# MLP products by one level of Strassen's algorithm, with the hidden activations kept in DRAM

## The chip, the core and the metric

One core of a Trainium2 chip runs the whole kernel. TensorE multiplies matrices out of SBUF into PSUM; VectorE (DVE), ScalarE (ACT) and GpSimd (POOL) work on tiles elementwise; SyncE (SP) issues most of the DMAs. The metric is the device time of one execution in microseconds, the median of several runs.

## What is computed

Two layers of a diffusion block on 512 latent and 256 context tokens of 1024 features in float32. Each layer has a mixer (recurrence, attention, pooling) and then the part that is changed, the MLP:

```python
def _mlp(h, w1, w2):
    return jnp.square(jax.nn.relu(h @ w1)) @ w2
...
        x = x + g2 * _mlp(_modulate(_rmsnorm(x, g_norm2[l]), sh2, sc2), w_ff1[l], w_ff2[l])
        if not last:
            h = h + cg1 * y_ctx
            h = h + cg2 * _mlp(_modulate(_rmsnorm(h, g_norm2[l]), csh2, csc2), w_ff1[l], w_ff2[l])
```

w_ff1 is 1024 x 4096 and w_ff2 4096 x 1024. Layer 0 carries 768 tokens through it, layer 1 (the last) only the 512 latent ones.

## The kernel before

Features lie on partitions, tokens in columns. Every float32 operand of a product is kept as two float32r parts, high (a cast) and low (the operand minus its high part), and a product is three matmuls: high x high, high x low, low x high (`mm3`, L241 is its matmul). The weights come as blocks of 128 x 1024 in the order of their use; `Weights.advance` loads a block ("raw"), ScalarE casts it to "whi" (L142) and VectorE subtracts to get "wlo" (L143).

`ffn(l)` runs the MLP in four groups of eight hidden chunks of 128 features. `ff1` makes a chunk: 8 feature tiles x 3 matmuls x 2 column segments (512 and 258 in layer 0; 256 and 258 in layer 1, two further columns carrying the shift), then VectorE multiplies by the tokens' 1/rms ("tf", L539), ScalarE takes ReLU (L544, L546) and the square ("hh", L1255), VectorE squares again and subtracts ("r" L1256, "hl" L1257). The hidden chunks stay in SBUF. `ff2` multiplies a group's eight chunks into each of the eight output tiles and VectorE adds the gated result to the residual tile "xo" out of PSUM (L1276). Both layers' `ffn` are straight code; a scheduler orders each engine's instructions, and each engine then runs its own in order.

Beside this, `mod_rows` (L413, "junk") computes the modulation of the next layer on VectorE, a row block at a time for both streams; these items ("fill") are spread over layer 0's MLP. In the mixer's tail ("wo" products, `add_to` L1189, `scaled` L467 and L468) GpSimd adds up squares ("acc", L456).

## Time and profile before

| | |
|---|---|
| median of 3 runs | 1652.8 us (1650.26 to 1652.82) |
| span of the profiled execution (the page gives no other time for it) | 1650.7 us |
| TensorE busy | 1582.8 us |
| VectorE busy | 1122.0 us |
| ScalarE busy | 680.4 us |
| GpSimd busy | 368.2 us |
| bytes read from and written to HBM | 170.90 and 12.12 MB |

Busy time is an average over stages with different limits, so the stages are read one by one: mixer of layer 0 up to 443 us, its MLP to 984, mixer of layer 1 to 1283, its MLP to the end. Only the last link of a chain of waits costs time.

### The profile page before, as it was taken

The page shows a single profiled execution, that of the slowest core. Times are in us where ns is not written, and L with a number is a line of the kernel's source. Part 1 is how long each engine was busy: PE and PEld are TensorE (multiplying, and loading weights), DVE is VectorE, ACT ScalarE, POOL GpSimd, SP SyncE. Part 2 cuts the span into 40 slices and gives each one's busy share as a digit, 9 for nine tenths or more (in the row PEclk, how much of TensorE's full clock was granted, in tenths as well). Part 3 has the DMA queues.
Part 4 walks back from the last instruction along what each step waited for, and adds up shares of the span by engine and source line. Part 5 has one row for each costly group of instructions (what it writes and reads, how often), then busy time and mean ns, then how long its engine had stood idle before and what let it go on. Part 6 is the DMA issues. An engine that isn't in the chain of part 4 may idle for free.

```text
span 1650.7 us, 24064 instructions
## 1 busy us (share of the span) xinstructions
PE 1582.8 (96%) x9519; PEld 1380.6 (84%) x9519; DVE 1122.0 (68%) x1810; ACT 680.4 (41%) x1078; POOL 368.2 (22%) x376
## 2 busy tenths in 40 slices
...
GB/s 251 198 150 185 81 58 37 94 185 152 82 97 144 142 89 119 187 78 128 166 90 120 142 109 21 121 71 20 97 122 141 103 90 96 97 90 93 100 27 102
DMA packets 54016, 184.57 MB, mean 112 GB/s; under 512 B 6624, under 2 KB 7264, under 8 KB 53904
## 3 DMA queue, kind: packets, MB, share of 16 engines
...
HBM read 170.90 MB, written 12.12 MB: 111 GB/s over the span
## 4 chain that ended last, share of the span: by engine, by line
PE 76%; DVE 15%; issue 4%; ACT 3%; POOL 1%; DMA 1%; SPq 0%; DVEq 0%; ACTq 0%; POOLq 0%
PE f L241 55%; PE wo L241 5%; PE inps L241 4%; PE sc L241 3%; DVE wlo L143 3%; PE tp L914 2%; DVE p L897 1%; PE modps L369 1%; DVE junk L413 1%; PE qp L241 1%; PE pv L936 1%; PE pv L937 1%; DVE ptl L922 1%; PE gps L241 1%; PE kns L823 1%
## 5 line engine op out<-in xcount | busy, mean ns | idle before, releaser
L142 ACT CAST whi<-raw 128x1024 fp32r<-128x1024 f32 x210 | 219.6, 1048 | 657.2 <-PE f L241 550.7
L143 DVE TENSOR_TENSOR wlo<-raw,whi 128x1024 fp32r<-128x1024 f32 x210 | 276.3, 1318 | 35.3 <-ACT whi L142 32.6
L241 PE MATMUL f<-xh,whi 128*128 128x258 f32 (+2 forms) x1024 | 234.6, 310 | 1.0 <-DVE tf L539 1.0
L241 PE MATMUL f<-xl,whi 128*128 128x258 f32 (+2 forms) x1024 | 234.5, 310 | 0.0
L241 PE MATMUL f<-xh,wlo 128*128 128x258 f32 (+2 forms) x1024 | 234.1, 310 | 0.0
L241 PE MATMUL f<-hh,wlo 128*128 128x512 f32 (+1 forms) x768 | 232.2, 356 | 0.0
L241 PE MATMUL f<-hl,whi 128*128 128x512 f32 (+1 forms) x768 | 231.9, 356 | 0.0
L241 PE MATMUL f<-hh,whi 128*128 128x512 f32 (+1 forms) x768 | 231.3, 356 | 0.0
L1276 DVE SCALAR_TENSOR_TENSOR xo<-f,mod,xo 128x512 f32<-128x512 f32 x96 | 60.5, 658 | 195.6 <-PE f L241 195.6
L413 DVE SCALAR_TENSOR_TENSOR junk<-modraw,cb 128x1024 bf16<-128x1024 f32 x128 | 161.8, 1275 | 21.9 <-DMA modraw<-in_wb_dram 21.5
L241 PEld LDWEIGHTS f<-xh,whi 128*128 128x128 f32 x1024 | 157.8, 189 | 12.5 <-PE f L241 1.2
L241 PEld LDWEIGHTS f<-xl,whi 128*128 128x128 f32 x1024 | 158.2, 189 | 11.4
L241 PEld LDWEIGHTS f<-xh,wlo 128*128 128x128 f32 x1024 | 157.9, 189 | 11.3
L539 DVE TENSOR_TENSOR tf<-f,rb 128x770 f32<-128x770 f32 (+1 forms) x64 | 52.8, 826 | 159.1 <-PE f L241 150.2
L241 PEld LDWEIGHTS f<-hh,whi 128*128 128x128 f32 x768 | 126.5, 188 | 22.4
L241 PEld LDWEIGHTS f<-hh,wlo 128*128 128x128 f32 x768 | 126.3, 188 | 22.5
L241 PEld LDWEIGHTS f<-hl,whi 128*128 128x128 f32 x768 | 126.4, 188 | 22.3
L463 POOL CAST xh<-mod 128x2 fp32r<-128x2 f32 x24 | 10.6, 441 | 466.8 <-PE f L241 466.8
L225 POOL TENSOR_SCALAR p<-p,sm 128x768 f32<-128x768 f32 (+1 forms) x80 | 70.4, 880 | 117.3 <-DVE sm L899 81.1
L241 PE MATMUL inps<-xh,whi 128*128 128x512 f32 (+1 forms) x352 | 87.3, 331 | 7.3 <-ACT xh L467 5.6
L305 ACT ACTIVATE p<-p,sm 128x768 f32<-128x768 f32 (+1 forms) x80 | 68.2, 853 | 57.4 <-DVE p L897 56.8
L241 PE MATMUL inps<-xl,whi 128*128 128x512 f32 (+1 forms) x352 | 86.4, 326 | 3.1 <-DVE xl L468 3.1
...
## 6 DMA issues: line engine op xcount, KB each, us to landing
raw<-in_wb_dram SPq DMA_DIRECT2D x212, 512.0 KB, 3.6
...
```

The source lines that it names most:

```text
L142: nc.scalar.copy(hi, raw)
L143: nc.vector.tensor_tensor(lo, raw, hi.bitcast(F32), ALU.subtract)
L225: return self.nc.gpsimd.tensor_scalar(out, in_, scale, 0.0, ALU.mult, ALU.add)
L241: nc.tensor.matmul(ps, lhsT=a[:, ca], rhs=b[:, cb], start=first and i == 0, stop=last and i == 2)
L305: ins = self.nc.scalar.activation(out, in_, func, **kw)
L369: nc.tensor.matmul(ps[0:4, :], lhsT=self.ct[:, kk * 2 + j, :], rhs=w[:, j * 512:(j + 1) * 512], start=(kk == 0 and j == 0 and i == 0), sto ...
L413: nc.vector.scalar_tensor_tensor(junk, r, 1.0, c, ALU.mult, ALU.mult, accum_out=acc[l, g][:, v * 16 + i:v * 16 + i + 1])
L539: nc.vector.tensor_tensor(t[:, 0:n], ps[:, o:o + n], self.rb[:, 0:n], ALU.mult)
L823: nc.tensor.matmul(ps[:, tt:tt + 7:6], lhsT=sq[:, tt * 128:(tt + 1) * 128], rhs=self.cst[:, CST_SELK:CST_SELK + 2], start=True, stop=True)
L897: nc.vector.tensor_scalar(p[:, 0:keys], s, rq[:, qt:qt + 1], None, ALU.mult, ALU.min, accum_out=nb)
L914: nc.tensor.transpose(ps[:, j * 256 + q * 128:j * 256 + (q + 1) * 128], ps2[q][:, kt * 128:(kt + 1) * 128], self.ident)
L1276: nc.vector.scalar_tensor_tensor(x[:, a:a + e], ps[:, a:a + e], mod[:, v, 8 + m:9 + m], x[:, a:a + e], ALU.mult, ALU.add)
```

## The change

The MLP's two products are each cut into 2 x 2 blocks: the features of the contraction in halves, the output features in halves, the tokens in halves. A classical product of such blocks takes 8 block products; the new class `FeedForward` takes 7 (Winograd's form of Strassen's algorithm), whose operands are blocks or sums of blocks. Sums and differences are formed in float32, and only then split into high and low part:

- `weight_ops` makes the seven left operands from two raw blocks, "ws" holding the sums. Four sums of 128 x 512 run on GpSimd. Each operand is cast by ScalarE (L1303) and its low part taken (L1304) by VectorE, or by GpSimd for operands 5, 3 and 4 in layer 0 and for 3 in layer 1. `Weights.advance` no longer splits MLP blocks.
- `stream_ops` does the same for activations ("xq" from the scaled x, "hq" from the hidden chunks), sums ("tt") on GpSimd, low parts on VectorE.
- 16 `Hidden` jobs a layer make two hidden chunks each; 8 groups of 4 `Output` jobs make the output, two chunks of either half of the hidden features at a time. A job's seven products are issued as 1, then 3 and 4 of the job before, then 6, 5, 2, 7; the operands of the next job are prepared between them.
- The products are put together while they leave PSUM: some accumulate there, some are copied by ScalarE or added by VectorE to "ya", "yb" or "yo" tiles.
- A hidden chunk, after ReLU and square, is written to DRAM ("hd", by a DMA issued from ScalarE) and read back ("hz") for the second product. x is kept in DRAM too ("xf") and added at the end.
- Modulation rows of the last layer that only the context would use are not computed (`streams`): 80 of the L413 operations fall into layer 0's MLP where 112 did.
- The order of the output projection's tiles becomes 0, 4, 1, 5, 2, 6, 3, 7 (`KORD`), so that tiles which are summed come in pairs.

```diff
-GF = 8
 NSK = 5
 FLOW = (
-    "a2 acc gate hh hl inv knsq latn lsq mix p ps2 pth ptl pvt qlh qll rb t th u yh ylru z",
-    "a2 gate hh hl latn lsq lxp mxl p ps2 pth ptl pvt qlh qll row sq t th u yl ylru z",
+    "a2 acc gate inv knsq latn lsq mix p ps2 pth ptl pvt qlh qll rb t th u yh ylru z xz ya yb rr hz yo tt",
+    "a2 gate latn lsq lxp mxl p ps2 pth ptl pvt qlh qll row sq t th u yl ylru z xz ya yb rr hz yo tt",
 )
 NSLOT, NFLOW = 29, 18
-NGF = D_FF // 128 // GF
+NCH = D_FF // 128
+UNITS = NCH // 2
+UG = 2
+NGROUP = UNITS // UG
+KORD = tuple(j + h * KD // 2 for j in range(KD // 2) for h in range(2))
+FIRST, LATER = (1, 6, 5, 2, 7), (3, 4)
...
+def streams(l, g):
+    return 1 if l == DEPTH - 1 and g else 2
...
-        names += [(l, "ff1", c) for c in range(D_FF // 128)]
-        names += [(l, "ff2", g, m) for g in range(NGF) for m in range(KD)]
+        names += [(l, "ff1", c) for c in range(NCH)]
+        names += [(l, "ff2", g, q, h) for g in range(NGROUP) for q in range(KD // 4) for h in range(2)]
...
+            if name[1] in ("ff1", "ff2"):
+                self.split += 1
+                continue
...
+    def get_raw(self, name):
+        if self.order is None:
+            self.asked.append(name)
+            return FAKE
+        assert self.order[self.at] == name, (self.order[self.at], name)
+        self.loads = 1 if self.order[min(self.at + 4, len(self.order) - 1)][1] in ("ff1", "ff2") else 3
+        self.advance(self.at)
+        self.at += 1
+        return self.raw.pop(name)
...
-            junk = self.sp.tile([128, 1024], BF16, tag="s", name="junk", bufs=NSLOT)
-            for v, c in enumerate(self.cb):
+            junk = self.sp.tile([128, 1024], BF16, tag="f", name="junk", bufs=NFLOW)
+            nv = streams(l, g)
+            for v, c in enumerate(self.cb[:nv]):
                 nc.vector.scalar_tensor_tensor(junk, r, 1.0, c, ALU.mult, ALU.mult,
...
-        def ff1_out(c, ps):
-            t = self.scaled_out(ps, ctx, "tf")
-            r = self.slot("r")
-            self.biased(t, (r[:, 0:L], r[:, L:T]), ctx, AF.Relu)
-            hi, lo = self.slot("hh", F32R), self.slot("hl", F32R)
-            nc.scalar.activation(hi[:, 0:n], r[:, 0:n], AF.Square)
-            nc.vector.tensor_tensor(r[:, 0:n], r[:, 0:n], r[:, 0:n], ALU.mult)
-            nc.vector.tensor_tensor(lo[:, 0:n], r[:, 0:n], hi[:, 0:n].bitcast(F32), ALU.subtract)
-            hid[c] = (hi, lo)
...
-            for j in range(GF):
-                wk = [t[:, j * 128:(j + 1) * 128] for t in w]
-                self.mm3(wk, hid[g * GF + j], segs, j == 0, j == GF - 1)
-            x = self.X[m]
-            mod = self.mod[l, 2].rearrange("p (v j) -> p v j", v=2)
-            for v, a, e in ((0, 0, L), (1, L, C))[:2 if ctx else 1]:
-                nc.vector.scalar_tensor_tensor(x[:, a:a + e], ps[:, a:a + e], mod[:, v, 8 + m:9 + m], x[:, a:a + e],
-                                               ALU.mult, ALU.add)
...
-        self.ffn(1)
+        self.ff.run()
...
+        slow = (5, 3, 4) if self.ctx else (3,)
+        self.low_w = {p: nc.gpsimd if p in slow else nc.vector for p in range(1, 8)}
+        self.jobs = [Hidden(self, u) for u in range(UNITS)]
+        self.jobs += [Output(self, g, m) for g in range(NGROUP) for m in range(KD // 2)]
...
+    def parts(self, hi, lo, src, eng):
+        self.nc.scalar.copy(hi, src)
+        eng.tensor_tensor(lo, src, hi.bitcast(F32), ALU.subtract)
...
+    def stream_ops(self, name, blocks, n, q):
+        nc, sub = self.nc, ALU.subtract
+        t = {}
+        def new(*p):
+            s = self.K.slot("tt")
+            for i, k in enumerate(p):
+                t[k] = s[:, i * n:(i + 1) * n]
+        def part(p, src=None):
+            q[p] = self.K.slot(name, F32R)
+            self.parts(q[p][:, 0:n], q[p][:, n:2 * n], t[p] if src is None else src, nc.vector)
+        def sums():
+            b11, b12, b21, b22 = blocks()
+            new(5, 6)
+            new(7, 4)
+            nc.gpsimd.tensor_tensor(t[5], b12, b11, sub)
+            nc.gpsimd.tensor_tensor(t[6], b22, t[5], sub)
+            nc.gpsimd.tensor_tensor(t[4], b21, t[6], sub)
+            part(6)
+        def third():
+            _, b12, _, b22 = blocks()
+            nc.gpsimd.tensor_tensor(t[7], b22, b12, sub)
+            part(7)
+        return [lambda: part(1, blocks()[0]), sums, lambda: part(5), lambda: part(2, blocks()[2]), third,
+                lambda: part(3, blocks()[3]), lambda: part(4)]
...
+    def weight_ops(self, names, w):
+        nc, K = self.nc, self.K
+        a, t = [], {}
+        def pair(*ps):
+            s = K.rawp.tile([128, 1024], F32, tag="ws", name="ws", bufs=2)
+            for i, p in enumerate(ps):
+                t[p] = s[:, i * 512:(i + 1) * 512]
+        def part(p, src=None):
+            w[p] = K.wp.tile([128, 1024], F32R, tag="w", name="wo")
+            self.parts(w[p][:, 0:512], w[p][:, 512:1024], t[p] if src is None else src, self.low_w[p])
+        def begin():
+            for name in names:
+                r = K.w.get_raw(name)
+                a.extend([r[:, 0:512], r[:, 512:1024]])
+            part(1, a[0])
+        def sums():
+            pair(5, 6)
+            nc.gpsimd.tensor_tensor(t[5], a[2], a[3], ALU.add)
+            nc.gpsimd.tensor_tensor(t[6], t[5], a[0], ALU.subtract)
+            part(6)
+        def third():
+            pair(7, 3)
+            nc.gpsimd.tensor_tensor(t[7], a[0], a[2], ALU.subtract)
+            nc.gpsimd.tensor_tensor(t[3], a[1], t[6], ALU.subtract)
+            part(7)
+        return [begin, sums, lambda: part(5), lambda: part(2, a[1]), third, lambda: part(3), lambda: part(4, a[3])]
...
+    def product(self, ps, p, lhs, rhs, n, start):
+        for i, ((wh, wl), q) in enumerate(zip(lhs, rhs)):
+            xh, xl = q[p][:, 0:n], q[p][:, n:2 * n]
+            for j, (a, b) in enumerate(((wh, xh), (wh, xl), (wl, xh))):
+                self.nc.tensor.matmul(ps, lhsT=a, rhs=b, start=start and i == 0 and j == 0,
+                                      stop=i == len(rhs) - 1 and j == 2, skip_group_check=True)
...
+        total = 7 * UNITS - 14
+        prev = None
+        for i, job in enumerate(self.jobs + [None]):
+            nxt = list(self.jobs[i + 1].prep) if i + 1 < len(self.jobs) else []
+            seq = [(job, p) for p in (FIRST if i else (1, 5, 6, 2, 7))] if job else []
+            late = [(prev, p) for p in LATER] if prev else []
+            seq = seq[:1] + late + seq[1:]
+            for at, (jb, p) in enumerate(seq):
+                jb.do(p)
+                if i == 0 and p == 6:
+                    r = K.norm_sums(self.ctx)
+                if i == 0 and p == 7:
+                    self.norm_spread(r)
+                upto = -(-len(nxt) // (len(seq) - at))
+                for step in nxt[:upto]:
+                    step()
+                del nxt[:upto]
+                ticks += 1
+                while ran < min(fills, -(-fills * ticks // total)):
+                    K.run_fill()
+                    ran += 1
+            prev = job
...
+        ff.product(ps, p, lhs, ff.xq, n, p in (1, 2, 5))
+        half = slice(0, n), slice(n, 2 * n)
+        if p == 1:
+            nc.scalar.copy(self.ya[:, half[0]], ps)
+        elif p == 6:
+            nc.scalar.copy(self.ya[:, half[1]], ps)
+        elif p == 5:
+            nc.scalar.copy(self.yb[:, half[1]], ps)
+        elif p == 2:
+            nc.vector.tensor_tensor(self.ya[:, half[0]], ps, self.ya[:, half[0]], ALU.add)
+        elif p == 7:
+            nc.vector.tensor_tensor(self.yb[:, half[1]], ps, self.yb[:, half[1]], ALU.add)
+        elif p == 3:
+            nc.vector.tensor_tensor(self.ya[:, half[1]], ps, self.ya[:, half[1]], ALU.add)
+            nc.vector.tensor_tensor(self.ya[:, 0:2 * n], self.ya[:, 0:2 * n], ff.rb[:, 0:2 * n], ALU.mult)
+            self.out(self.u, self.ya)
+        else:
+            nc.vector.tensor_tensor(self.yb[:, half[0]], ps, ff.rb[:, half[0]], ALU.mult)
+            nc.vector.tensor_tensor(self.yb[:, half[1]], self.yb[:, half[1]], ff.rb[:, half[1]], ALU.mult)
+            self.out(self.u + UNITS, self.yb)
+    def out(self, c, y):
+        ff, K, nc = self.ff, self.ff.K, self.ff.nc
+        r = K.slot("rr")
+        for at, e, v, t in ff.pieces(2):
+            nc.scalar.activation(r[:, t:t + e], y[:, at:at + e], AF.Relu, bias=y[:, ff.nh + v:ff.nh + v + 1])
+        nc.scalar.activation(r[:, 0:ff.n], r[:, 0:ff.n], AF.Square)
+        nc.scalar.dma_start(out=K.hd[ff.l, c, :, 0:ff.n], in_=r[:, 0:ff.n])
...
+        for t in range(UG):
+            c = (m % 2 * UG + t) * 128
+            lhs.append((self.w[p][:, c:c + 128], self.w[p][:, 512 + c:512 + c + 128]))
+        ff.product(ps, p, lhs, [ff.hq[g * UG + t] for t in range(UG)], n, p in (1, 2, 5))
+        a, b = slice(0, n), slice(n, 2 * n)
+        y, o = {1: (m, a), 6: (m, b), 7: (m + 4, b), 5: (m + 4, b), 2: (m, a), 4: (m + 4, a), 3: (m, b)}[p]
+        y = ff.y[y][:, o]
+        if g == 0 and p in (1, 6, 5, 4):
+            nc.scalar.copy(y, ps)
+        else:
+            nc.vector.tensor_tensor(y, ps, y, ALU.add)
```

GpSimd's instructions in the middle of layer 0's MLP. Before, there are none between the memset of "rb" and the first scaled tiles of the next layer, apart from those of the mixer's last tiles:

```order
L463 CAST xh<-mod_1_975 128x2
L464 TENSOR_TENSOR xl<-mod_1_975,xh 128x2
L507 MEMSET rb 128x2
L463 CAST xh<-mod_1_975 128x2
L464 TENSOR_TENSOR xl<-mod_1_975,xh 128x2
L456 TENSOR_TENSOR acc<-acc,sq 128x768
```

After, the same engine in the first product of layer 0, one job and the start of the next ("ws" are sums of weight blocks, "wo" the split operands):

```order
L1359 TENSOR_TENSOR ws<-raw 128x512
L1365 TENSOR_TENSOR ws<-raw 128x512
L1360 TENSOR_TENSOR ws<-ws,raw 128x512
L1366 TENSOR_TENSOR ws<-raw,ws 128x512
L1304 TENSOR_TENSOR wo<-ws,wo 128x512 x2
L1304 TENSOR_TENSOR wo<-raw,wo 128x512
L1359 TENSOR_TENSOR ws<-raw 128x512
L1365 TENSOR_TENSOR ws<-raw 128x512
```

Seven operations of 512 columns per job stand where the engine had nothing to do.

VectorE in the first product of layer 0, before: one chunk and the start of the next.

```order
L539 TENSOR_TENSOR tf<-f_6098,rb 128x770
L143 TENSOR_TENSOR wlo<-raw,whi 128x1024
L413 SCALAR_TENSOR_TENSOR junk,modr_0_5644<-modraw,cb_1664 128x1024
L1256 TENSOR_TENSOR r<-r 128x768
L413 SCALAR_TENSOR_TENSOR junk,modr_0_5644<-modraw,cb_1665 128x1024
L1257 TENSOR_TENSOR hl<-r,hh 128x768
L539 TENSOR_TENSOR tf<-f_6168,rb 128x770
```

After, one job (two chunks); f is a PSUM tile, every other operand lies in SBUF:

```order
L1472 TENSOR_TENSOR ya<-f_6527,ya 128x386
L1304 TENSOR_TENSOR wo<-raw,wo 128x512
L1474 TENSOR_TENSOR yb<-f_6250,yb 128x386
L1481 TENSOR_TENSOR yb<-yb,rb 128x386
L1476 TENSOR_TENSOR ya<-f_6250,ya 128x386
L1477 TENSOR_TENSOR ya<-ya,rb 128x772
L1304 TENSOR_TENSOR wo<-ws,wo 128x512
L1304 TENSOR_TENSOR wo<-raw,wo 128x512
```

The additions out of PSUM now stand in one queue with low parts and scalings of SBUF operands.

VectorE in the second product of layer 1. Before, one low part of weights and one addition per output tile alternate:

```order
L143 TENSOR_TENSOR wlo<-raw,whi 128x1024
L1276 SCALAR_TENSOR_TENSOR xo<-f_13978,mod_2_8145,xo 128x512
L143 TENSOR_TENSOR wlo<-raw,whi 128x1024
L1276 SCALAR_TENSOR_TENSOR xo<-f_14010,mod_2_8145,xo 128x512
L143 TENSOR_TENSOR wlo<-raw,whi 128x1024
```

After:

```order
L1561 TENSOR_TENSOR yo<-f_17492,yo 128x256
L1561 TENSOR_TENSOR yo<-f_17557,yo 128x256
L1304 TENSOR_TENSOR hq<-hz,hq 128x256
L1304 TENSOR_TENSOR wo<-ws,wo 128x512
L1304 TENSOR_TENSOR hq<-tt,hq 128x256
L1561 TENSOR_TENSOR yo<-f_17651,yo 128x256
L1561 TENSOR_TENSOR yo<-f_17557,yo 128x256
L1304 TENSOR_TENSOR hq<-tt,hq 128x256
L1561 TENSOR_TENSOR yo<-f_17701,yo 128x256
L1304 TENSOR_TENSOR wo<-raw,wo 128x512
```

Each of the seven products of a job has its own addition, and the low parts of weights and hidden activations stand between them.

## Rows read from the trace of the kernel before

**Rows 1.** The page, busy time, share of the span and instructions of each engine.

```profile
PE 1582.8 (96%) x9519; PEld 1380.6 (84%) x9519; DVE 1122.0 (68%) x1810; ACT 680.4 (41%) x1078; POOL 368.2 (22%) x376
```

**Rows 2.** The chain of waits in both MLPs: start us, us, what.

```profile
443.34 8.46 PE f L241 x48
...
459.44 525.02 PE f L241 x2992
...
1297.24 349.30 PE f L241 x2208
```

**Rows 3.** Windows (A:B us, length): busy time per engine, PEclk granted, DMA share, GB/s.

```profile
443.00:984.00 541.00, 541.00 (x3091) 473.62 (x3091) 338.29 (x480) 147.21 (x189) 28.14 (x30) 1.00 0.39 123
1283.00:1646.50 363.50, 362.48 (x2318) 328.10 (x2316) 166.86 (x196) 106.59 (x131) 1.52 (x2) 1.00 0.28 88
...
1300.00:1336.00 36.00, 36.00 (x305) 36.00 (x304) 21.62 (x27) 13.99 (x18) 0.00 (x0) 1.00 0.27 94
1340.00:1376.00 36.00, 36.00 (x157) 29.30 (x156) 12.87 (x14) 6.32 (x7) 0.00 (x0) 1.00 0.32 103
```

**Rows 4.** ScalarE's groups by shape: xcount, busy us, mean ns, idle before.

```profile
L216 ACT CAST pth<-tp 128x512 fp32r<-128x512 f32 x72 | 42.2, 586 | 12.4 <-PE tp L914 11.2
L216 ACT CAST pth<-tp 128x256 fp32r<-128x256 f32 x64 | 23.9, 373 | 13.0 <-DVE ptl L922 9.9 <-PE tp L914 2.9
L546 ACT ACTIVATE r<-tf 128x256 f32<-128x256 f32 x32 | 15.8, 494 | 0.0
```

**Rows 5.** GpSimd's groups by shape.

```profile
L212 POOL TENSOR_TENSOR kb<-kb,kx 128x768 f32<-128x768 f32 x8 | 14.5, 1831 | 6.6 <-DMA kb<-kd 6.6
L212 POOL TENSOR_TENSOR ql<-qf,qh 128x512 fp32r<-128x512 f32 x8 | 10.3, 1286 | 5.5 <-ACT qh L216 5.4
```

**Rows 6.** VectorE back to back, timeline: start us, us, engine, line, operation.

```profile
600.37 0.95 DVE L1256 TENSOR_TENSOR r<-r 128x768 f32<-128x768 f32 x1
601.24 1.22 DVE L413 SCALAR_TENSOR_TENSOR junk<-modraw,cb 128x1024 bf16<-128x1024 f32 x1
...
602.38 0.95 DVE L1257 TENSOR_TENSOR hl<-r,hh 128x768 fp32r<-128x768 f32 x1
```

**Rows 7.** GpSimd in layer 0's mixer, timeline.

```profile
35.86 2.51 POOL L456 TENSOR_TENSOR acc<-acc,sq 128x768 f32<-128x768 f32 x1 [9.57 <-ACT sq L447]
...
38.45 2.73 POOL L456 TENSOR_TENSOR acc<-acc,sq 128x768 f32<-128x768 f32 x1
...
41.26 2.69 POOL L456 TENSOR_TENSOR acc<-acc,sq 128x768 f32<-128x768 f32 x1
```

**Rows 8.** VectorE at the same time, timeline.

```profile
36.68 2.77 DVE L143 TENSOR_TENSOR wlo<-raw,whi 128x1024 fp32r<-128x1024 f32 x1
...
44.86 1.22 DVE L143 TENSOR_TENSOR wlo<-raw,whi 128x1024 fp32r<-128x1024 f32 x1
```

**Rows 9.** GpSimd at the end of layer 1's mixer, timeline.

```profile
1278.96 1.30 POOL L456 TENSOR_TENSOR acc<-acc,sq 128x512 f32<-128x512 f32 x1 [3.83 <-ACT sq L447]
```

**Rows 10.** VectorE there, timeline.

```profile
1276.13 0.74 DVE L468 SCALAR_TENSOR_TENSOR xl<-xo,s,xh 128x512 fp32r<-128x512 f32 x1
...
1279.25 1.55 DVE L468 SCALAR_TENSOR_TENSOR xl<-xo,s,xh 128x512 fp32r<-128x512 f32 x1
```

**Rows 11.** VectorE in layer 1's attention, an operand (qp) in PSUM, timeline.

```profile
1220.50 0.68 DVE L865 TENSOR_TENSOR qf<-qp,tq 128x512 f32<-128x512 f32 x1
```

**Rows 12.** GpSimd at that time, timeline.

```profile
1220.39 1.85 POOL L212 TENSOR_TENSOR kel<-kb,keh 128x768 fp32r<-128x768 f32 x1
```

**Rows 13.** Windows of the mixers: columns as in rows 3.

```profile
0.00:320.00 320.00, 280.49 (x1581) 225.14 (x1582) 268.09 (x480) 193.09 (x319) 151.04 (x143) 0.90 0.40 134
984.00:1283.00 299.00, 278.01 (x1752) 245.33 (x1752) 244.12 (x446) 165.19 (x301) 138.19 (x141) 0.98 0.26 86
```

271 lines of the change are left out of this document (174 added, 97 removed).

## The prediction

> **What bounds the kernel now.** The page comes first. TensorE is busy for 96% of the span, VectorE 68%, GpSimd 22% [rows 1]. Those are averages over stages, so the chain of waits is read next, for the two feed-forward stretches alone: it is one unbroken run of matmuls in each, 525.02 us for 2992 and 349.30 us for 2208 [rows 2]. [...]
>
> **What it removes.** A duration in the rows (a 512-column matmul "394 ns") is longer than its share of the pace, because matmuls are pipelined; the pace is a stretch over its count. In layer 0 that is 525.02 / 2992 = 175.5 ns at 384.5 columns on average [rows 2]. In layer 1 it is 36.00 / 304 = 118.4 ns at 257 columns and 36.00 / 157 = 229 ns at 512 [rows 3] (a window also counts the matmuls that its ends cut). Before, layer 0 has 3072 of these matmuls, layer 1 1536 narrow and 768 wide ones. After, each layer has 16 x 7 x 4 x 3 = 1344 for the first product and 8 x 4 x 7 x 2 x 3 = 1344 for the second, of 386 and 384 columns in layer 0, 258 and 256 in layer 1. Layer 0: 3072 x 0.1755 = 539.1 becomes 2688 x 0.1755 = 471.7, which is 67.4 us less. Layer 1: 1536 x 0.1184 + 768 x 0.229 = 357.7 becomes 2688 x 0.1184 = 318.3, 39.4 us less. TensorE's saving is 107 us if nothing else sets the pace.
>
> **What it adds, engine by engine.** Each of 32 sets of weights per layer now needs 7 casts (ScalarE), 7 low parts and 4 block sums at 512 columns; each of 20 sets of activations (4 of x, 16 of the hidden layer) 7 casts, 7 low parts and 4 sums at half the tokens. Sums are GpSimd's, and so are 3 of the 7 low parts of the weights in layer 0, 1 of 7 in layer 1.
>
> ScalarE has room. In the tightest stage, a first-product unit of layer 1 (TensorE 84 x 0.1184 = 9.9 us), it has 3 copies and 7 casts, 4 ReLUs of 256 columns and 2 squares of 512: 3 x 0.373 + 7 x 0.586 + 4 x 0.494 + 2 x 0.586 = 8.4 us [rows 4]. The hidden activations go to DRAM and back: 32 x 384 KB and 32 x 256 KB each way, 42 MB, some 47 GB/s over 904 us beside the 88 to 123 GB/s of now, with DMA engines 28 to 39% busy [rows 3]. I cost the transfers at nothing: a unit is read long after it is written, except at the last group.
>
> GpSimd's price: 1.286 us at 512 columns, 1.831 at 768, thus 2.13 ns a column, 1.013 us at 384 and 0.74 at 256 [rows 5]. Layer 0: 32 x 7 = 224 at 512 and 80 at 384 or 386 make 288.1 + 81.0 = 369.1 us. Layer 1: 32 x 5 = 160 and 80 make 205.8 + 59.2 = 265.0. Alone this would fit under 471.7 and 318.3.
>
> VectorE's price: back to back, an operation of 768 columns starts 0.87 us before the next and one of 1024 columns 1.14 us [rows 6]; on that line 512 columns take 0.60, 384 take 0.465, 256 take 0.33. It nearly fits as well: a group of the second product in layer 1 (4 jobs, TensorE 168 x 0.1184 = 19.9 us) has 28 additions out of PSUM, 12 low parts of weights and 14 of activations, 9.2 + 7.2 + 4.6 = 21.0 us, 1.1 over; in layer 0 it is 13.0 + 4.8 + 6.5 = 24.3 of 29.5.
>
> **The two engines do not fit together.** At 35.86 us GpSimd adds up three 768-column tiles while VectorE forms low parts, the same operation on the same kinds of operands as every low part in the change. GpSimd's operation takes 1.83 us alone [rows 5]; here the three take 2.51, 2.73 and 2.69, and VectorE's low part takes 2.77 instead of 1.22 [rows 7, 8]. From 38.45 to 41.26, 2.81 us, there was one of each: 1.83 + 1.14 = 2.97 in turn. So they do not overlap; they alternate, and the hand-over saves 0.16 us, 5%. The end of layer 1's mixer shows who yields: GpSimd starts at 1278.96 and takes its usual 1.30, VectorE's operation at 1279.25, usually 0.74, takes 1.55 [rows 9, 10]. An operation with one operand in PSUM is not touched: 0.68 us at 512 columns while GpSimd runs its usual 1.85 [rows 11, 12]. [...]
>
> So GpSimd's work and VectorE's work on two SBUF operands have to be added. VectorE's part, layer 0: low parts of weights 128 x 0.60 = 76.8, of activations 140 x 0.465 = 65.1, scaling by 1/rms 16 x (0.875 + 0.465) = 21.4, the modulation rows (junk, now 80 in these 14 units) 80 x 1.14 = 91.2; 254.5. Layer 1: 192 x 0.60 + 140 x 0.33 + 16 x (0.61 + 0.33) = 176.4. With GpSimd: 623.6 and 441.4. The four sets of x fall into the mixer's tail: 16 x 1.013 + 28 x 0.465 = 29.2 and 21.1 off. There remain 594.4 + 420.3 = 1014.7 us, against 791 of TensorE and 904.5 of now. By stage, shared against TensorE: first product of layer 0 18.4 against 14.7 a unit (mean), second 37.4 against 29.5 a group; layer 1 11.0 against 9.9 and 30.6 against 19.9. It decides in all four, hence the whole stretch goes by it: **+110 us**.
>
> Bounds of that term. Below: every hand-over saves 5% and the shared port never rests, 0.95 x 1014.7 = 964, +59. Above: the engines work in order with short buffers (two "ws" tiles, ten "w" tiles of which a set holds seven), GpSimd waits for casts, VectorE's low parts stand ahead of the additions that free PSUM; nothing in the trace shows such a stage, so I allow a tenth of the time with the port idle, 1015 / 0.9 = 1127, +223. I take 1015, saving and idling against each other.
>
> **Ends.** Now the first f matmul follows the last wo at 443.34 at once [rows 2]. After, the last pair of x tiles needs scaling, three sums of 1.013 us behind an addition of 1.8 and a cast before the second product can run: I take 5 us a layer, and 5 for the last tiles, which finish in twos. An extreme is 0 and 30. The 48 modulation operations that go (1.14 us each, 55 us of VectorE) are already missing from the sum. The mixers keep their work.
>
> **Sum.** 1650.7 (span) + 110 + 15 = 1776. The median of the runs lies 2 us above that span, so 1778 us.
>
> **The rivals.** *TensorE keeps the pace* (0.14, faster). If VectorE and GpSimd slip past each other, as operations out of PSUM do [rows 11, 12], the pace is 791: 1650.7 - 107 + 15 = 1559. It decides when the shared work costs less than 889 us, an eighth less than my sum; the hand-over gives only 5%, and 18 to 37 us of shared work a unit or group leaves no second place to hide it. For it: most of GpSimd's operations of this trace run at their own pace (1.286 us is a mean) [rows 5].
> *Starved TensorE* (0.08, slower still). VectorE loses the port twice in a row, PSUM is freed late, TensorE idles and its clock falls. In the first 320 us, with TensorE busy 88%, the granted clock is 0.90; in layer 1's mixer, busy 93%, 0.98 [rows 13]. At 0.90 TensorE would need 791 / 0.9 = 879, still under 1015, so the clock alone costs nothing; it counts where stalls and clock add up, beyond 1127: 1890 to 2000.
> *They meet* (0.03, same): the shared work costs 880 to 895 and the time stays at 1650.
>
> **How the numbers follow.** My forecast (port-bound, 0.75) is 1778, its own range 1705 (0.95 x 1015, ends at 0) to 1890 (1127, ends 15). Between it and the faster rival lie cases in which low parts partly fit beside GpSimd. To leave out no more than two in ten I go down to 1640 and up to 1895: below stay 0.13, above 0.07. What a measurement can tell from no change is about 0.2%, 3 us (the runs lie between 1650.26 and 1652.82). Faster by more 0.14, within 0.03, slower 0.83.
>
> **What the next profile would show.** Right: in the feed-forward stretches GpSimd is busy most of the time, near 600 and 420 us long; VectorE's 512-column low parts average above 0.8 us and GpSimd's 512-column operations above 1.29; additions out of PSUM, narrower than the one of [rows 11], stay under its 0.68; TensorE's idle time there sums to 200 us and ends on casts, low parts or sums. The wider gap is in layer 1's second product. [...]

## The result, and the profile after

The changed kernel takes 1942.24 us (median of 4 runs, 1938.46 to 1946.08) where the kernel before took 1652.81 on the same chip: 1.1755 times as long, 95% interval 1.1733 to 1.1778. The forecast was 1778, slower by 125 us; it is slower by 290, beyond the range, inside the band of the rival called starved TensorE.

The page of the changed kernel, busy time and share of the span (1936.4 us), beside [rows 1]:

```profile
PE 1614.7 (83%) x9519; PEld 1453.0 (75%) x9519; DVE 1607.4 (83%) x2538; ACT 968.9 (50%) x1888; POOL 1114.3 (58%) x920
```

Windows of the changed kernel, columns as in [rows 3]: the start of layer 0's MLP, its first and second product, the mixer of layer 1, and layer 1's two products.

```profile
443.00:471.00 28.00, 11.93 (x57) 9.87 (x56) 19.92 (x24) 14.02 (x30) 16.73 (x19) 0.79 0.36 129
471.00:790.00 319.00, 263.71 (x1332) 249.85 (x1332) 276.00 (x341) 150.52 (x301) 201.82 (x129) 0.93 0.56 189
784.00:1129.00 345.00, 281.26 (x1416) 258.07 (x1414) 300.70 (x417) 145.47 (x275) 249.25 (x193) 0.93 0.30 102
1129.00:1446.00 317.00, 276.57 (x1714) 242.36 (x1714) 260.48 (x467) 172.69 (x332) 156.95 (x156) 0.95 0.27 90
1446.00:1683.00 237.00, 195.89 (x1386) 190.88 (x1386) 163.73 (x222) 134.16 (x287) 140.75 (x107) 0.88 0.35 118
1683.00:1932.00 249.00, 194.28 (x1314) 175.23 (x1314) 225.09 (x401) 100.72 (x219) 152.08 (x123) 0.92 0.29 95
```

From its first to its last matmul, layer 0's MLP takes 658 us (541 before, forecast 594), layer 1's 485 (363.5 before, forecast 420): 1143 where the forecast had 1015. Around them the span has grown by 47 us where the forecast had 15: the first product of layer 0 starts at 471, not at 443, layer 1's mixer lasts 317 us, not 299, and under 1 us is at the end. 1143 - 904.5 + 47 = 286, the difference of the two spans (904.5 is 541.0 + 363.5, the two windows of [rows 3]).

The costliest groups of VectorE and GpSimd by line: operations, busy us, mean ns of one, idle before and its releasers.

```profile
L1561 DVE TENSOR_TENSOR yo<-f,yo 128x384 f32<-128x384 f32 (+1 forms) x416 | 193.5, 482 | 48.5 <-PE f L1376 45.8
L1304 DVE TENSOR_TENSOR wo<-raw,wo 128x512 fp32r<-128x512 f32 x160 | 184.6, 1155 | 45.2 <-ACT wo L1303 42.3 <-PE f L1376 1.5
...
L1304 DVE TENSOR_TENSOR wo<-ws,wo 128x512 fp32r<-128x512 f32 x160 | 151.2, 949 | 24.3 <-ACT wo L1303 22.3
...
L1366 POOL TENSOR_TENSOR ws<-raw,ws 128x512 f32<-128x512 f32 x64 | 101.8, 1591 | 1.3
L1360 POOL TENSOR_TENSOR ws<-ws,raw 128x512 f32<-128x512 f32 x64 | 101.4, 1585 | 2.0
```

The prediction's signs of its own theory are there, with one exception: low parts of 512 columns last 949 to 1155 ns (above 0.8 us), GpSimd's 512-column operations 1585 to 1591 (1286 in [rows 5]), additions out of PSUM 482 on average (under 0.68). TensorE's idle time before the two products sums to 214 us (200 said), but it ends mostly on the additions that free PSUM (L1561 83.2, L1480 38.2 us) and not on casts, low parts or sums. And the granted clock in the MLP windows is 0.88 to 0.93, where it was 1.00 [rows 3]; near 0.5 it stands only in short stretches (3.6 us at 0.53 in the job below). Middle stretches of the four products, same columns, show who is full:

```profile
560.00:760.00 200.00, 169.15 (x881) 160.84 (x881) 174.04 (x218) 92.78 (x183) 119.72 (x73) 0.96 0.62 212
800.00:1100.00 300.00, 249.73 (x1270) 230.58 (x1269) 257.78 (x364) 120.72 (x230) 218.69 (x165) 0.94 0.27 93
1500.00:1640.00 140.00, 120.77 (x869) 118.67 (x867) 94.22 (x124) 79.60 (x163) 79.24 (x53) 0.89 0.36 121
1700.00:1900.00 200.00, 152.37 (x1008) 136.81 (x1007) 187.66 (x331) 81.44 (x176) 134.14 (x109) 0.91 0.28 91
```

In the last row VectorE is busy 94% of the time, which counts in that its low parts of 512 columns last 860 to 1087 ns there (0.69 us where GpSimd is idle): it sets the pace. In the third nobody is full: TensorE 86%, VectorE 67%, GpSimd 57%, and that is the stage furthest from its forecast (237 us, forecast 176). One of its jobs, 13.8 us, in three windows:

```profile
1602.60:1606.20 3.60, 3.60 (x19) 3.60 (x19) 1.74 (x3) 2.36 (x6) 0.54 (x1) 0.53 0.53 171
1606.20:1614.60 8.40, 8.11 (x67) 7.89 (x66) 5.56 (x9) 4.54 (x9) 5.30 (x4) 1.00 0.24 83
1614.60:1616.40 1.80, 0.17 (x1) 0.17 (x2) 1.80 (x3) 0.87 (x3) 1.80 (x2) 1.00 0.38 146
```

TensorE idles at the end, as it does for 1.93 us ahead of the job, and the job begins with 3.6 us at a granted clock of 0.53: 19 matmuls there, 189 ns each, against 125 ns in the 8.4 us behind, at 1.00. The chain of waits through that job (start us, us, what):

```profile
1602.39 6.12 PE f L1376 x36
...
1608.91 0.53 ACT wo L1303
...
1609.47 1.01 DVE wo L1304
1610.48 0.34 DVE ya L1476
1610.81 0.07 DVE wo L1304
1610.88 1.22 issue
...
1614.38 1.39 issue
1615.77 0.42 DVE yb L1480
```

The next product waits for L1480, which frees its PSUM bank, and L1480 stands in VectorE's queue behind low parts, which wait in turn for casts on ScalarE (L1303). The two "issue" pieces of 1.2 and 1.4 us lie inside such low parts. VectorE, GpSimd and TensorE at these places, timeline:

```profile
1610.01 1.63 POOL L1360 TENSOR_TENSOR ws<-ws,raw 128x512 f32<-128x512 f32 x1
...
1610.74 1.45 DVE L1304 TENSOR_TENSOR wo<-ws,wo 128x512 fp32r<-128x512 f32 x1
...
1614.03 1.27 POOL L1365 TENSOR_TENSOR ws<-raw 128x512 f32<-128x512 f32 x1
1614.28 1.56 DVE L1304 TENSOR_TENSOR wo<-raw,wo 128x512 fp32r<-128x512 f32 x1 [1.49 <-ACT wo L1303]
...
1616.23 1.03 PE L1376 MATMUL f<-xq,wo 128*128 128x258 f32 x4 [1.93 <-DVE yb L1480]
```

Both low parts begin inside a GpSimd operation and last 1.45 and 1.56 us, where two of the same job with GpSimd idle (1605.97 and 1607.75 us) last 0.69; TensorE idles for 1.93 us behind the second, which had waited 1.49 us for its cast before.

### The profile page after: what moved, and what is told of

Its sections match the earlier page's. It is cut to its first block, busy times and chain, and to the rows that moved or that the text cites. A ratio compares the mean times of both kernels' runs of the same rounds, so it can differ in the third digit from the quotient of the medians.

```text
span 1936.4 us, 26854 instructions
## 1 busy us (share of the span) xinstructions
PE 1614.7 (83%) x9519; PEld 1453.0 (75%) x9519; DVE 1607.4 (83%) x2538; ACT 968.9 (50%) x1888; POOL 1114.3 (58%) x920
## 4 chain that ended last, share of the span: by engine, by line
DVE 34%; PE 28%; issue 8%; ACT 5%; DMA 4%; POOL 3%; DVEq 0%; ACTq 0%; SPq 0%; POOLq 0%
PE f L1376 17%; DVE wo L1304 8%; DVE hq L1304 6%; DVE yo L1561 4%; DVE junk L439 4%; PE wo L266 3%; DMA raw<-in_wb_dram 2%; ACT wo L1303 2%; DVE xq L1304 2%; PE inps L266 2%; DVE ya L1477 2%; PE sc L266 2%; PE tp L941 1%; DMA modraw<-in_wb_dram 1%; ACT rr L1488 1%
## 5 line engine op out<-in xcount | busy, mean ns | idle before, releaser
L1376 PE MATMUL f<-hq,wo 128*128 128x384 f32 (+1 forms) x2688 | 468.6, 330 | 120.5 <-DVE yo L1561 83.2
L1376 PEld LDWEIGHTS f<-hq,wo 128*128 128x128 f32 x2688 | 426.4, 201 | 161.9 <-DVE yo L1561 112.8
L1376 PE MATMUL f<-xq,wo 128*128 128x386 f32 (+1 forms) x2688 | 457.3, 333 | 93.9 <-DVE yb L1480 35.9
L1376 PEld LDWEIGHTS f<-xq,wo 128*128 128x128 f32 x2688 | 437.9, 207 | 112.1 <-DVE yb L1480 40.1
L1303 ACT CAST wo<-ws 128x512 fp32r<-128x512 f32 x256 | 155.3, 618 | 225.5 <-PE f L1376 123.8
L1304 POOL TENSOR_TENSOR wo<-ws,wo 128x512 fp32r<-128x512 f32 x96 | 152.2, 1586 | 172.9 <-ACT wo L1303 150.8
L1561 DVE TENSOR_TENSOR yo<-f,yo 128x384 f32<-128x384 f32 (+1 forms) x416 | 193.5, 482 | 48.5 <-PE f L1376 45.8
L1304 DVE TENSOR_TENSOR wo<-raw,wo 128x512 fp32r<-128x512 f32 x160 | 184.6, 1155 | 45.2 <-ACT wo L1303 42.3
L1359 POOL TENSOR_TENSOR ws<-raw 128x512 f32<-128x512 f32 x64 | 94.9, 1483 | 153.9 <-issue 78.4
L1304 DVE TENSOR_TENSOR wo<-ws,wo 128x512 fp32r<-128x512 f32 x160 | 151.2, 949 | 24.3 <-ACT wo L1303 22.3
L1303 ACT CAST wo<-raw 128x512 fp32r<-128x512 f32 x192 | 118.1, 617 | 88.8 <-PE f L1376 87.6
L157 DVE TENSOR_TENSOR wlo<-raw,whi 128x1024 fp32r<-128x1024 f32 x82 | 122.7, 1506 | 13.8 <-ACT whi L156 13.8
L1304 DVE TENSOR_TENSOR hq<-tt,hq 128x384 fp32r<-128x384 f32 (+1 forms) x128 | 104.5, 826 | 4.7 <-ACT hq L1303 4.7
L1360 POOL TENSOR_TENSOR ws<-ws,raw 128x512 f32<-128x512 f32 x64 | 101.4, 1585 | 2.0
L1366 POOL TENSOR_TENSOR ws<-raw,ws 128x512 f32<-128x512 f32 x64 | 101.8, 1591 | 1.3
L1365 POOL TENSOR_TENSOR ws<-raw 128x512 f32<-128x512 f32 x64 | 93.6, 1463 | 3.8 <-DVE wo L1304 1.7
```

The costliest lines, as they stand in the source:

```text
L157: nc.vector.tensor_tensor(lo, raw, hi.bitcast(F32), ALU.subtract)
L1303: self.nc.scalar.copy(hi, src)
L1304: eng.tensor_tensor(lo, src, hi.bitcast(F32), ALU.subtract)
L1359: nc.gpsimd.tensor_tensor(t[5], a[2], a[3], ALU.add)
L1360: nc.gpsimd.tensor_tensor(t[6], t[5], a[0], ALU.subtract)
L1365: nc.gpsimd.tensor_tensor(t[7], a[0], a[2], ALU.subtract)
```

## The experiments

Pace, here and below, is the mean time between the starts of matmuls in the trace, over the stretch from 20% to 85% of a stage's matmuls, times the matmuls of a job of the first product or of a group of the second. The last column is both MLPs, first to last matmul, to within 1 us. Each ratio is to the kernel before on the same chip.

| kernel | median us | ratio to before, 95% | layer 0 job, group | layer 1 job, group | MLPs us |
|---|---|---|---|---|---|
| forecast | 1778 | | 18.4, 37.4 | 11.0, 30.6 | 1015 |
| the change | 1942.2 | 1.1755 (1.1733 to 1.1778) | 19.6, 38.5 | 13.55, 32.6 | 658 + 485 |
| e1_psum_low | 1828.3 | 1.1057 (1.1036 to 1.1078) | 18.7, 34.4 | 10.84, 27.9 | 600 + 411 |
| e2_vector_only | 1834.9 | 1.1093 (1.1063 to 1.1123) | 17.7, 37.7 | 10.89, 31.2 | 615 + 438 |
| e3_no_sums | 1732.1 | 1.0479 (1.0459 to 1.0499) | 17.1, 32.4 | 10.85, 25.0 | 574 + 391 |
| e4_third_bank | 1928.1 | 1.1674 (1.1652 to 1.1696) | 20.8, 38.6 | 12.45, 32.9 | 662 + 475 |
| e5_fill_spread | 1943.4 | 1.1748 (1.1709 to 1.1788) | 16.3, 46.0 | 13.55, 33.0 | 661 + 486 |
| e6_first_only | 1700.7 | 1.0289 (1.0269 to 1.0308) | 16.1, 33.6 | 10.87, 22.7 | 551 + 366 |
| e7_one_matmul | 1862.9 | 1.1269 (1.1239 to 1.1299) | 18.8, 39.2 | 10.54, 31.4 | 620 + 433 |
| e8_adds_to_scalar | 1888.7 | 1.1426 (1.1403 to 1.1449) | 19.6, 34.7 | 13.15, 27.9 | 632 + 455 |
| e9_classical | 1691.4 | 1.0223 (1.0204 to 1.0241) | 17.0, 33.6 | 11.55, 22.7 | 551 + 372 |
| e10_sync_store | 1943.7 | 1.1761 (1.1743 to 1.1779) | 19.7, 38.7 | 13.54, 33.3 | 658 + 489 |
| e11_spare_matmuls | 1935.0 | 1.1707 (1.1691 to 1.1723) | 20.1, 38.5 | 12.39, 32.3 | 662 + 478 |

### Do the two engines alternate?

```diff
+    def pool_two(i):
+        nc.gpsimd.tensor_tensor(g[i], a, b, ALU.add)
...
+    def dve_two(i):
+        nc.vector.tensor_tensor(v[i], c, d, ALU.subtract)
```

> A kernel of its own that computes none of the reference: twelve phases of ten operations each on 128 x 512 float32 tiles, GpSimd and VectorE alone and then side by side. Alone I expect the prices of the prediction: GpSimd 1.29 us, VectorE 0.60 to 0.70 us, with two SBUF operands or with one in PSUM. Side by side with two SBUF operands each: if the engines alternate, as the prediction took it, each of VectorE's ten operations lasts about 1.9 us (its own 0.6 and one of GpSimd's 1.29) and GpSimd's stretch to the same. If GpSimd keeps the port as long as its next operation is ready, GpSimd's ten take 12.9 us as alone, one operation of VectorE lasts near 13 us, and the other nine 0.6. With an operand in PSUM, or with one operand only, VectorE should be as alone under both. Where GpSimd waits for ScalarE before each operation, VectorE should get in at each gap under both.

Timeline: GpSimd's ten operations with two SBUF operands and VectorE's, each stretch x10; then VectorE's ten with an operand in PSUM (kp), first with GpSimd idle at the start (23.29), then beside GpSimd's operations with two SBUF operands (64.39); last its ten with one operand, beside GpSimd's with one (127.43) and with GpSimd idle.

```profile
4.70 15.82 POOL L34 TENSOR_TENSOR g<-ga,gb 128x512 f32<-128x512 f32 x10 [4.26 <-ACT gb L31]
...
6.73 14.94 DVE L47 TENSOR_TENSOR v<-va,vb 128x512 f32<-128x512 f32 x10 [5.33 <-ACT vb L31]
23.29 6.06 DVE L50 TENSOR_TENSOR v<-va,kp 128x512 f32<-128x512 f32 x10 [1.61 <-ACT va L31]
...
64.39 6.07 DVE L50 TENSOR_TENSOR v<-va,kp 128x512 f32<-128x512 f32 x10 [9.64 <-ACT va L31]
...
66.90 12.01 POOL L37 TENSOR_TENSOR g<-g,gb 128x512 f32<-128x512 f32 x9
...
127.43 6.83 DVE L53 TENSOR_SCALAR v<-va 128x512 f32<-128x512 f32 x10 [7.72 <-ACT va L31]
134.95 3.44 DVE L53 TENSOR_SCALAR v<-va 128x512 f32<-128x512 f32 x10 [0.68 <-ACT va L31]
```

They alternate. "The port", in what follows, is a name for whatever makes them take turns; the runs show the turns and not what makes them. In the common stretch of the first pair the trace's single records show one GpSimd and one VectorE operation every 1.667 us; alone GpSimd starts one every 1.22 us and VectorE every 0.60, together 1.82. The hand-over saves 8.4%, not 5%. With an operand in PSUM VectorE needs 6.07 us for ten beside GpSimd, 0.60 each, and 6.06 with GpSimd idle at the start. With a single SBUF operand it does collide, against the expectation: 6.83 us for ten beside GpSimd, 3.44 without.

### Take the shared port away, in three ways

e1_psum_low (the zeros take one of the four PSUM tiles of 512 columns):

```diff
+        if eng is self.nc.vector:
+            eng.tensor_tensor(lo, hi.bitcast(F32), self.K.kps[:, 0:lo.shape[1] if self.K.w.order is not None else 1], ALU.subtract)
+        else:
+            eng.tensor_tensor(lo, src, hi.bitcast(F32), ALU.subtract)
```

> VectorE's low parts of weights and activations take their subtrahend's partner from a PSUM tile of zeros, so that they have one SBUF operand; their number, place in the queue and width stay (their values do not: the low parts of these operands are replaced by the negated high parts). The port theory (VectorE loses the port to GpSimd for whole runs of operations): the 949 to 1155 ns of a 512-column low part fall to about 0.6, and with GpSimd's 353 and 250 us then colliding with scalings and modulation rows alone, TensorE comes near its own pace: 1590 to 1700 us. The rival, that the loss comes from the order (additions out of PSUM queued behind low parts that wait for casts, short buffers, raw loads): the durations fall but the waits stay, 1850 us or more.

e2_vector_only, the same edit in all eight sums:

```diff
-        slow = (5, 3, 4) if self.ctx else (3,)
+        slow = ()
...
-            nc.gpsimd.tensor_tensor(t[5], b12, b11, sub)
+            nc.vector.tensor_tensor(t[5], b12, b11, sub)
```

> All block sums and low parts move to VectorE; GpSimd has nothing in the MLPs. VectorE's work by the prices of the prediction: about 15.9 us a unit of the first product in layer 0 and 36 us a group of the second, 9.2 us a unit in layer 1 and 29 a group. The port theory: nothing contends, VectorE's own sum or TensorE decides stage by stage, 16 x 15.9 + 8 x 36 = 542 and 16 x 9.9 + 8 x 29 = 390, so 1650.7 - 904.5 + 932 + some 30 at the ends, 1690 to 1730 us, less than the change although one engine does the work of two. The order theory: more stands ahead of each addition out of PSUM, so it becomes worse than the change, over 1950.

e3_no_sums, the sums of weights; those of activations likewise:

```diff
-            pair(5, 6)
-            nc.gpsimd.tensor_tensor(t[5], a[2], a[3], ALU.add)
-            nc.gpsimd.tensor_tensor(t[6], t[5], a[0], ALU.subtract)
+            t[5], t[6], t[7], t[3] = a[2], a[3], a[0], a[1]
```

> The block sums are left out (an operand that should be a sum is one of its blocks instead), casts, low parts, matmuls and additions stay. GpSimd keeps 3 of 7 low parts of the weights in layer 0 and 1 of 7 in layer 1, about 124 and 41 us. The port theory: shared work is 378 and 217 us, below TensorE's 472 and 318, so the time comes to 1560 to 1650. The order theory: casts and low parts still stand in the same queues, so most of the loss stays, over 1800.

All three fall between the two theories. The port is dear: moving GpSimd's work onto VectorE, which was the busier of the two, makes the kernel 107 us faster, and in layer 1's first product each of the three brings a job from 13.55 to 10.84 to 10.89 us. In e1 a low part of 512 columns of weights lasts 683 ns, so the edit does free it; but its MLPs are 132 us shorter than the change's and its start and layer 1's mixer 22 us longer. None comes down to its port forecast (1700, 1730, 1650 at most), so the port is not all. What stays is seen in e3, where sums cost nothing; a window in layer 1's second product:

```profile
1550.00:1700.00 150.00, 132.49 (x998) 121.88 (x999) 136.07 (x319) 76.00 (x156) 15.84 (x12) 1.00 0.34 114
```

Neither VectorE (91%) nor TensorE (88%) is full, at a granted clock of 1.00, and yet a group takes 25.0 us where the prediction's prices are 21.0 for VectorE and 19.9 for TensorE. The price of an addition is not the reason: back to back the 28 additions of a group start 0.34 us apart (0.33 in the prediction). In layer 0's first product of e3 the largest shares of the chain are the modulation rows (22.5%) and the weights' loads (19.7%).

### More PSUM, and the modulation rows moved

e4_third_bank:

```diff
-            self.bank = K.psA("f1")
+            if self.u % 3 == 2:
+                self.bank = K.psB("f1"), K.psB("f1")
+            else:
+                t = K.psA("f1")
+                self.bank = t[:, 0:512], t[:, 512:1024]
```

> The change with a third pair of PSUM banks for the jobs of the first product (every third job takes two single tiles instead of a double one), so that a job's first product waits for the additions of the job three back, not two back; nothing else moves. In the change a job of layer 1's first product takes 13.83 us, of which TensorE idles 1.93 before a bank is free and then runs a stretch at half clock. Theory that PSUM is freed late because additions stand in VectorE's queue behind low parts: the idle and its half-clock stretch go, layer 1's first product falls from 237 us to 185 to 200 and layer 0's by some 10 to 20, 1870 to 1900 us in all. Rival, that the shared port itself sets the pace there: VectorE is as late as before, the wait only moves to operands that are not ready, under 15 us less in all.

e5_fill_spread:

```diff
-        total = 7 * UNITS - 14
+        total = 7 * (UNITS + NGROUP * KD // 2) - 28
```

> The change with the modulation rows spread over both products of layer 0 instead of the first alone; the work is the same. Theory that the first product of layer 0 is held by these rows (91 us of VectorE and their loads beside the weights, in a stage whose forecast was 294 us and which took 340): it falls to 290 to 305, and the second product, where VectorE and the port are full, takes what was moved and rises from 319 by 25 to 45, so that the whole changes by less than 20 us. Rival, that the weights' loads alone hold it: the first product stays above 325 us.

The third pair gives 1.1 us of the 3 in layer 1's job, nothing in layer 0, and 14 us in all, as the rival said: lateness of the bank is a part of it, a small one. The wait moves to operands that are not ready: from 1500 to 1640 us the weight loads of TensorE wait 18.2 us for casts (L1303), where in the change none of their waits ends on a cast. Spreading the rows takes the first product of layer 0 from 339 to 293 us and adds as much behind; the MLP stays at 661. What VectorE and GpSimd have to do in layer 0 is one account: where it stands does not matter.

### Who sets the pace: TensorE taken out, additions taken out

e7_one_matmul (the products lack the two matmuls with low parts):

```diff
-            for j, (a, b) in enumerate(((wh, xh), (wh, xl), (wl, xh))):
+            for j, (a, b) in enumerate(((wh, xh),)):
```

> The change with one matmul of three in the MLPs' products (high by high; the two matmuls with low parts are left out, the low parts are still formed). TensorE has a third of its work there and can't set the pace. Theory that VectorE and GpSimd set the pace by themselves: both MLPs take as long as in the change within some 5%, 1100 to 1145 us instead of 1143, in all 1880 to 1940. Starved TensorE, whose idle stretches and half clock add to theirs: the time falls to 1800 or less, first of all in layer 1's first product, where a job takes 13.55 us and should come to 11 or less.

e8_adds_to_scalar, the same edit in four places:

```diff
-            nc.vector.tensor_tensor(y, ps, y, ALU.add)
+            nc.scalar.copy(y, ps)
```

> The change with VectorE's additions out of PSUM replaced by copies on ScalarE (the products of a block are not added up). Prediction's sum (only GpSimd's work and VectorE's work on two SBUF operands count, the additions lie beside GpSimd's): no gain, 1920 us or more, a group of layer 1's second product stays near 32.6 us. Theory that VectorE's whole queue counts, additions included, and then its waits for the port: VectorE loses 28 additions of 0.415 us a group there (11.6 us) and waits more often for the port, so that a group falls to 28 to 30 us and all to 1830 to 1890.

A window of e7 in layer 1's first product:

```profile
1460.00:1600.00 140.00, 84.29 (x368) 74.05 (x368) 137.29 (x158) 100.88 (x211) 98.60 (x64) 0.66 0.47 151
```

VectorE is busy for 98% of it (67% in the change): without TensorE's load VectorE and GpSimd set the pace, at 18.8, 39.2, 10.54 and 31.4 us, where the prediction's shared sum said 18.4, 37.4, 11.0 and 30.6. Both MLPs take 1053 us, 38 over the forecast and 90 under the change. So both theories hold a part: the shared sum is what it was said to be, and TensorE adds 90 us to it although its own work fits below. Who waits for whom in layer 1's first product of the change (1500 to 1640 us; us in all, times, longest):

```profile
ACT wo L1303 <- PE f L1376: 27.3, 32, 1.7
DVE wo L1304 <- ACT wo L1303: 24.5, 30, 1.5
...
PE f L1376 <- DVE yb L1480: 19.2, 10, 1.9
DVE ya L1472 <- ACT ya L1466: 16.3, 10, 2.1
```

That is a ring. TensorE waits for VectorE to free a bank, VectorE for ScalarE's casts and copies, and ScalarE's casts for TensorE, since they write into the ten "w" tiles, of which a set holds seven. In e7 VectorE's waits come to 2.3 us in 140. More "w" tiles were not tried. The stretch between the MLPs was 13 us longer here than in the change, for which I have no reason.

e8 tells how the sum came out right. Without additions a group of layer 1's second product takes 27.9 us, which is 30.6 less the 8.4% of the hand-over (28.0); in layer 0 34.7, where 37.4 less 8.4% is 34.3. With additions it is 32.6 and 38.5. Operations with an operand in PSUM do not collide with GpSimd (in m1_port ten take 6.07 us beside it, and 6.06 with it idle at the start), yet these additions are not free: 4.7 and 3.8 us a group. By the single records the port is in use (a GpSimd operation or a VectorE operation on SBUF operands alone is under way) for 98% of a window of e8 in that product (1690 to 1860 us) and for 88% of the change's (1700 to 1900): while VectorE adds, GpSimd is not always there to use the port.

### Is the half clock a cost of its own?

```diff
+            if ff.last and self.u:
+                spare = K.psB("spare")
+                for k in range(16):
+                    nc.tensor.matmul(spare[:, 0:n], lhsT=ff.jobs[self.u - 1].w[7][:, 0:128], rhs=ff.xq[0][1][:, 0:n], start=True,
+                                     stop=True, skip_group_check=True)
```

> The change with 16 matmuls of 258 columns more per job in layer 1's first product, into a PSUM tile that nothing reads; 13 of them stand just ahead of the product that waits 1.93 us for its bank, 3 one product earlier. TensorE gets 19% more work there (1.9 us a job). If the half clock that follows the idle is a cost of its own: the granted clock stays near 1.00 there, and a job takes 12.0 to 12.8 us instead of 13.55, 12 to 25 us less in all, with more work. If the clock costs nothing, since VectorE and GpSimd are as late as before: a job takes 13.5 or more.

A window in the same product, and the piece of the chain that opens a job there (in the change 6.12 us):

```profile
1500.00:1640.00 140.00, 137.53 (x1117) 135.28 (x1116) 102.19 (x135) 87.82 (x177) 87.47 (x57) 1.00 0.38 131
```

```profile
1582.83 4.62 PE f L1376 x36
```

It is. With 19% more matmuls a job takes 12.39 us instead of 13.55, at a granted clock of 1.00 instead of 0.89; the 36 matmuls that open a job take 4.62 us. The whole kernel is 7 us faster than the change, and so is the stage, where 12 to 25 were expected: the first three jobs took 6 us longer, for a reason that is not shown.

The change alone shows the same. Its timeline of TensorE, a job's 84 matmuls in a row:

```profile
1494.71 10.41 PE L1376 MATMUL f<-xq,wo 128*128 128x258 f32 x84 [1.93 <-DVE yb L1480]
1507.06 11.93 PE L1376 MATMUL f<-xq,wo 128*128 128x258 f32 x84 [1.93 <-DVE yb L1480]
...
1534.73 10.42 PE L1376 MATMUL f<-xq,wo 128*128 128x258 f32 x84 [1.92 <-DVE yb L1480]
```

Each begins after the same idle. Over the first and the third the granted clock is 1.00, over the second 0.86; of the twelve such idles from 1494 to 1644 us nine are followed by a stretch at half clock. So a slow job of 13.85 us is 10.4 us of matmuls, 1.5 us for the half clock and 1.9 us of idle, and the spare matmuls give back what the clock costs. The idle is as long behind a fast job as behind a slow one: the ring of waits follows TensorE.

### The starts of the layers

Four VectorE operations at the layer starts of the change last 3.4 to 8.9 us, where 0.4 to 0.7 is usual. One of them, VectorE's timeline:

```profile
1449.15 7.62 DVE L1304 TENSOR_TENSOR xq<-xz,xq 128x258 fp32r<-128x258 f32 x1 [2.45 <-ACT xq L1303]
```

GpSimd had issued two DMAs just before (1446.34 to 1447.54 us) and began its run of operations at once. Two kernels of their own looked into it.

```diff
+    def dma(k):
+        for j in range(k):
+            nc.gpsimd.dma_start(out=out[j], in_=raw)
```

> A kernel of its own that computes none of the reference: runs of ten GpSimd operations of 512 columns, beside five VectorE operations with two SBUF operands that become ready during the run; in some phases GpSimd issues one or two DMAs just before the run, in some the operations are chained or alternate between 512 and 258 columns. In the change four VectorE operations of 0.4 to 0.7 us lasted 3.4 to 8.9 us, each in a run of GpSimd that followed a DMA which GpSimd had issued; the first experiment shows strict alternation without one. If the DMA is the reason, the phases with a DMA show an operation of 5 us or more and those without show 1.2 to 1.8 us. If the mixed widths are the reason, only the last two phases show it. If neither, all alternate.

One operation lasted 11.38 us, in the one run that GpSimd began 0.1 us behind its DMA issue; where 0.27 us or more lay between, the engines alternated. The next kernel has the DMAs right ahead of each of its first six runs:

> A kernel of its own that computes none of the reference: twelve runs of ten GpSimd operations of 512 columns, six after two DMAs issued by GpSimd and six without, VectorE's three operations of 258 columns becoming ready later from run to run. In the second kernel of its own one VectorE operation lasted 11.38 us, through a whole run, and the others alternated. If a DMA that GpSimd has just issued is what bars VectorE, the operations of 3 us or more stand in the first six runs alone, at the shorter delays; if it is where in a GpSimd operation VectorE comes, they stand in both halves; if neither is seen, the reason stays open.

```diff
+        for j in range(k):
+            nc.gpsimd.dma_start(out=out[j], in_=b)
+        for i in range(N):
+            nc.gpsimd.tensor_tensor(g[i], a, b, ALU.add)
+        for i in range(3):
+            q(i)
```

Timeline: two of the runs with DMA issues ahead, the last two rows one without; VectorE's three operations stand in one row, and the first takes nearly all of it.

```profile
19.91 1.10 POOL L38 DMA_DIRECT2D out_dram<-gb  x2 [1.47 <-ACT gb L32]
21.03 12.22 POOL L40 TENSOR_TENSOR g<-ga,gb 128x512 f32<-128x512 f32 x10
21.34 12.88 DVE L45 TENSOR_TENSOR r<-va,vb 128x258 fp32r<-128x258 f32 x3 [1.93 <-ACT va L36]
...
79.11 1.09 POOL L38 DMA_DIRECT2D out_dram<-gb  x2 [1.47 <-ACT gb L32]
80.22 12.23 POOL L40 TENSOR_TENSOR g<-ga,gb 128x512 f32<-128x512 f32 x10
82.87 10.54 DVE L45 TENSOR_TENSOR r<-va,vb 128x258 fp32r<-128x258 f32 x3 [4.26 <-ACT va L36]
...
93.76 12.79 POOL L40 TENSOR_TENSOR g<-ga,gb 128x512 f32<-128x512 f32 x10 [1.31 <-ACT gb L32]
94.69 3.43 DVE L45 TENSOR_TENSOR r<-va,vb 128x258 fp32r<-128x258 f32 x3 [1.28 <-ACT va L36]
```

Six of six runs behind a DMA issue bar VectorE to their end, whenever it comes; six of six without one alternate. In the change the DMAs are those that store x.

Then the change without these DMAs on GpSimd:

```diff
-        nc.gpsimd.dma_start(out=K.xf[self.l, m, :, 0:self.n], in_=x[:, 0:self.n])
+        nc.sync.dma_start(out=K.xf[self.l, m, :, 0:self.n], in_=x[:, 0:self.n])
```

> The change with the stores of x to DRAM issued by SyncE instead of GpSimd; nothing else moves. In the kernel of its own with varied delays, every run of GpSimd that followed its DMA issues without a pause barred VectorE to the run's end (9.9 to 13.1 us), and no run without them did. In the change VectorE operations of 6.14, 8.92, 3.43 and 7.62 us stand at the two layer starts, right after such issues. If these holds are what makes the starts dear: they vanish, the starts shorten by 10 to 25 us in all, 1917 to 1932 us. If the starts are long for another reason (sums, casts and low parts one behind the other): the long operations vanish, but the time stays within 5 us.

The long operations at the layer starts are gone, the time is not: 1943.7 us, the first product of layer 0 starts at 471.2 (470.8 in the change). The holds lay beside other waits; they are not what makes the starts dear.

### Is there a better version?

e6_first_only makes the second product from four plain operands in eight block products; e9_classical does so for both.

```diff
+        if not strassen:
+            return [begin, lambda: part(2, a[1]), lambda: part(3, a[2]), lambda: part(4, a[3])]
```

> Seven block products for the first product alone, with all sums and low parts on VectorE and the third pair of PSUM banks; the second product in the classical eight block products (four plain operands a set, two products accumulated in PSUM before an addition), the modulation rows spread over both products. GpSimd has nothing in the MLPs. Port theory with VectorE's prices: first products near TensorE's pace, 250 and 178 us, second near that of before, 275 and 185, ends 30: 1650.7 - 904.5 + 888 + 30, 1640 to 1690 us. If order and latency keep the first products where they are with VectorE alone (302 and 194 us): 1710 to 1740.

> The new structure (jobs, hidden activations by way of DRAM, output tiles in pairs, modulation rows spread over both products) with the classical eight block products in both MLP products: four plain operands a set, no sums, low parts on VectorE, GpSimd with nothing in the MLPs. It tells what the structure costs without the seven products. If the ends alone are dear (the 28 us before the first product of layer 0 and 18 more in layer 1's mixer come from the structure): 1680 to 1700 us. If they come from the sums and low parts at the start: 1655 to 1670.

No version beats the kernel before. e9 is 2.2% slower: its MLPs take 551 + 372 us where 541 + 363.5 stood, its first product starts at 450.3 us, 7 late, and layer 1's mixer lasts 310 us, 11 more. That is the price of the structure without a single sum. Seven products for the first product save 6 us of MLP against it (551 + 366) and lose more around it, 9 us over e9 in all: 1700.7, between the two times expected. In e9 TensorE is busy throughout a window of layer 1's first product (1330 to 1480 us, 1249 matmuls), 0.120 us each, so 84 of them are 10.1 us; a job of e6 takes 10.87, with TensorE busy 96% (1370 to 1500 us).

## Why the prediction was wrong

**What bounds the kernel now, what TensorE saves.** The reading of before holds: in both MLPs TensorE sets the pace and GpSimd, busy for 28.1 and 1.5 us [rows 3], has room. The saving of 107 us is never seen, since TensorE does not set the pace of the whole in any stage of the change. Its own price was right within 2%: 10.1 us a job of layer 1 by the matmuls of e9, where the prediction had 9.9. Even where VectorE and GpSimd hold it little (e1, e2, e3, e6) a job takes 10.84 to 10.89.

**The shared port: 1015 us, right within 4%, partly by luck.** With TensorE taken out the MLPs take 1053 us, stage by stage within 5%; as a term that is +149 beside the +110 of the sum. Two errors in it cancel: the hand-over saves 8.4%, some 85 us of 1015, where I set saving against idling, and the additions that I held to be free cost 4.7 us a group in layer 1 and 3.8 in layer 0, 68 us in all. What the remaining 38 us consist of was not taken apart. No run shows the shared port of the bounds as such; what they show is turns, one operation of each engine every 1.667 us in m1_port, and none with an operand in PSUM (6.07 us for ten beside GpSimd, 6.06 with it idle at the start).

**The step that failed: "It decides in all four, hence the whole stretch goes by it", and with it "so the clock alone costs nothing".** I took the shared sum and TensorE's work as two limits of which the larger decides, with TensorE's lost clock hidden under the larger, and left what lies beyond to a rival at 0.08. The runs showed that they add up, by 90 us over both MLPs (1143 against 1053 in e7), which puts the MLPs above my own upper bound of 1127. Where it was taken apart, in layer 1's first product, VectorE with GpSimd needs 10.5 us a job (e7) and TensorE's 84 matmuls take 10.4 at full clock; together they take 13.55: 10.4 of matmuls, 1.9 of idle, and in nine jobs of twelve 1.5 of half clock. The engines wait for each other in a ring within each job, so none of them is full, and the port rests for 24% of the time there, by the single records (8, 15 and 12% in the middle stretches of the other three products), where I had allowed a tenth. Spare matmuls in the idle give the clock's part back, a third bank 1.1 us. By the lengths of the stages the 90 us are 38 in this product, 13 in layer 0's first, and 24 and 16 in the two second products, with small overlaps. How much of these other parts is idling and how much clock was not taken apart.

**The ends, 15: 47.** The structure alone (e9) has 7 + 11, e3 without the sums 10 + 7, e2 with the sums on VectorE 15 + 10, the change with the sums on GpSimd 28 + 18. So the greater part comes with the sums on GpSimd ahead of the first product; GpSimd's DMA holds are ruled out (e10).

**The miss in one sum.** From 1778 to 1942 are 164 us: 38 of shared work, 90 that TensorE adds, 32 at the ends, and 4 by which the median stands further above the profiled span than I took. Three slips change nothing of this: 32 modulation operations go and not 48 (112 less 80), the range's lower end by its own terms is 1712 and not 1705, and the first rival's pace of 791 makes 1552 and not 1559.

**ScalarE and the transfers.** ScalarE has room, 57% busy in the third of the middle stretches, but it is not free: VectorE's low parts wait 24.5 us for casts in those 140 us. Transfers at nothing was too kind to layer 0's first product, which now moves 212 GB/s beside 123 before [rows 3] and where GpSimd waits for weights (32.8 us from 571 to 790 us); by how much was not separated from the modulation rows.
